# Roots written as transposes, alternating row groups and a reordered start of a hybrid encoder layer

## The chip, the cores and the metric

The kernel runs on one core of a Trainium2 chip. A core has five engines that run side by side, each with its own instruction queue: TensorE (PE, matrix products into the accumulation memory PSUM), VectorE (DVE), ScalarE (ACT), GpSimd (POOL) and SyncE (SP), which here issues all the transfers between the large memory and the on-chip memory. The metric is the device time of one execution in microseconds; the time before is the median of three runs.

## The reference

One inference step of one encoder layer, for a prompt of 2048 new tokens and for a sample of 32 next tokens that sees 2048 cached keys and values. All data are 32-bit floats.

```python
m, k, v, h_fin, ssm_conv_new = mixer(rmsnorm(x, p['g_mix_pre']), k_past, v_past, ssm_h0, ssm_conv_prev, p)
x = x + rmsnorm(m, p['g_mix_post'])
f, ffn_conv_new = conv_ffn(rmsnorm(x, p['g_ffn_pre']), ffn_conv_prev, p)
x = x + rmsnorm(f, p['g_ffn_post'])
```

The mixer projects the normalised tokens (1024 wide) once, to q, k, v, a gate z, the state-space inputs x, B, C and a step size dt. Group A is attention with stick-breaking weights, 8 heads of 64:

```python
log_keep = jnp.where(causal, jax.nn.log_sigmoid(-z), 0.0)
log_after = lax.cumsum(log_keep, axis=3, reverse=True) - log_keep
w = jnp.where(causal, jnp.exp(jax.nn.log_sigmoid(z) + log_after), 0.0)
```

Group B is a state-space scan, 8 heads of 64 in 2 groups, after a causal convolution of width 4 and a SiLU (y times sigmoid of y) on x, B and C. Both outputs are normalised, concatenated and sent through one output projection. The feed-forward part has a hidden width of 2816, a causal convolution of width 3 on the gate branch and a GeLU gate. An RMS norm divides by the root of a token's mean square. Keys, values and states are outputs too.

## The kernel before, in words

Tokens lie along the free dimension and features on the 128 partitions. The 2080 tokens are cut into four chunks (512, 512, 512 and 544, the last with the 32 of the sample behind the prompt's). Every dense product is computed as three products of a high and a low part (`dense`, line 180): high by high, high weight by low input, low weight by high input. A weight comes in raw (`raw`), is cast to its high part on ACT (line 160), has its low part subtracted on POOL (line 161), and is stored to a scratch area (line 164) from which later chunks recall it (line 152).

The first stage, `phase_in`, takes the four chunks s = 0 to 3 in turn. For each chunk:

- The six groups of 128 state-space inputs are projected, copied out of PSUM on ACT (line 412), convolved on DVE (lines 421 and 425) and sent through SiLU (`silu`, lines 397 and 398: a sigmoid on ACT and a product on DVE). The SiLU of a group is owed: it is issued behind the copy of the next group, and the last one behind the first copies of v.
- v and dt are projected in blocks of 128 tokens (line 452, two halves of 260 columns), copied out on ACT (line 459 in the first chunk, 461 in the others), split into high and low parts on POOL (lines 473 and 474, one buffer), and sent out by two kinds of transfer (`o_v`, line 468, and `vS`, line 476). In the first chunk v's weights are loaded before this by `load_wv` in four pieces through one raw buffer (lines 301 to 303: load, cast on ACT, subtraction on DVE). In the later chunks, ahead of the blocks b = 0, 1 and 2, one weight of the output projection each is loaded, split and stored for later use, eight in all.
- The state-space scan runs over blocks of 128 tokens. Line 540 multiplies C and B, line 542 the incoming state by C, each for the two groups g, whose operands lie on partitions 0 to 63 and 64 to 127; the two groups write different banks of the tile `cy`. A 32-bit product that isn't marked for the fast format makes two passes on PE, which the trace shows as two records.
- The next chunk's tokens are loaded (line 318; for chunk 1 the loads are put behind the last raw weight load so far, `kn.load`), normalised, and k and q are projected. In this stage three buffers hold split weights and two hold raw ones.

Then follow the four attention stages, `heads(s)`. A stage walks over slots (head, key chunk, block of 128 queries): scores into PSUM (lines 910 to 914), two sigmoids on ACT (758, 759), a product scan on DVE (761), a product (766), transposes on PE (929), a split on ACT and DVE (933, 934) and the product with v (951). The work of a slot's second half comes two slots behind its scores. Between slots a filler hands out steps of other dense work, at a steady rate that is counted in `debt`. In stage 0 the filler is the last chunk's gate z and its norm, and a generator `sample` is advanced every third slot: it takes the sample's 2048 cached keys in chunks kc = 3 to 0 (and the 32 new ones, kc = 4), loads values (`sv`) and keys (`sk`), makes the scores of two pairs of heads g (line 809), and adds to the sum (line 825). In the stages 1 to 3 the filler is `Tail.stream` of the chunk before: output projection, residual, feed-forward part and final norm; the last chunk's follows alone.

The root of a norm is made in `rstd_steps`: the squares are summed over partitions per token into a column (line 222), the column gets its power of -1/2 on POOL (line 245), and one product per block of 128 tokens (line 257) turns it into rows that are the same on all partitions. The column, repeated over 128 columns, is one operand, the identity matrix the other.

Within each engine's queue the order is set by a planner that takes the program's order as priority and its own estimate of times; `kn.behind(a, b)` and `kn.pin` add edges that keep an instruction behind another.

Of the kernel before, what the change touches and what calls it, by code (L numbers as in the profile page):

```python
# [8 lines left out]
F32 = mybir.dt.float32  # L9
# [8 lines left out]
LOOK = 2  # L18
# [14 lines left out]
P = 128  # L33
D = 1024
KC = D // P
# [4 lines left out]
DH = 64  # L40
# [30 lines left out]
class Kernel:  # L71
# [139 lines left out]
    def rstd_steps(self, pool, psp, pt, sq, n, width, tag="rstd", out=None, rcol=None, of=None, stay=False, pin=False):  # L211
# [3 lines left out]
        nc = self.nc  # L215
# [32 lines left out]
        v = w  # L248
# [3 lines left out]
        for b in range(nb):  # L252
            q = min(P, n - b * P)
            if b == 4:
                nc.scalar.copy(r[:, :512], ps[:])
            c0 = b % 4 * P
            mm = nc.tensor.matmul(
                ps[:, c0 : c0 + q], v[:, b : b + 1].to_broadcast([P, P]), self.ident[:, :q], start=True, stop=True
            )
            if pin and b == 0:  # L260
                self.pin(mm)
        if pin:
# [9 lines left out]
def phase_in(kn, ctx):  # L272
# [8 lines left out]
    wp = kn.wp  # L281
# [16 lines left out]
    def load_wv():  # L298
        for k in range(0, KC, 2):
            raw = ep.tile([P, 2, 520], F32, name="wvraw")  # L300
            nc.sync.dma_start(raw[:], a["wv"][:, k : k + 2, :])
            nc.scalar.copy(wv[0][:, k : k + 2, :], raw[:])
            nc.vector.tensor_tensor(
                wv[1][:, k : k + 2, :], raw[:], wv[0][:, k : k + 2, :].bitcast(F32), op=ALU.subtract
            )
# [70 lines left out]
    for s, (t0, nt) in enumerate(SBS):  # L376
# [12 lines left out]
        if last:  # L389
            nc.vector.tensor_copy(  # L390
                raw[:, :, 515:518], kn.cv[:, C_SST : C_SST + 18].rearrange("p (c t) -> p c t", t=3)
            )
        owed = None

        def silu(y, copy):
            t = tmp.tile([P, 550], F32, name="t")
# [5 lines left out]
        for c, then in zip(order, (*order[1:], None)):  # L402
            if w is None:
                w = kn.weight(wp, a["wbx"][c], key=("bx", c))
            ahead = None
            if s == 0 and then is not None:
                ahead = kn.weight(wp, a["wbx"][then], key=("bx", then))
            for c0, c1 in tiles_of(nt):
                ps = psd.tile([P, 512], F32, name="o")
                kn.dense(ps, w, xs, c0, c1)  # L410
                e = min(c1, 512)
                copy = nc.scalar.copy(raw[:, c, 3 + c0 : 3 + e], ps[:, : e - c0])
                if ahead is not None:
                    kn.behind(copy, kn.cast)
                if c1 > 512:
                    copy = nc.scalar.copy(raw[:, c, 518:550], ps[:, e - c0 : c1 - c0])
            if s == 0:
                nc.vector.tensor_tensor(raw[:, c, 3 : 3 + nt], raw[:, c, 3 : 3 + nt], r0[:, :nt], op=ALU.mult)
            y = xc[:, c, :W] if c < 4 else bc[:, c - 4, :W]
            wc = C_SW + c * 4  # L420
            nc.vector.tensor_scalar(
                y, raw[:, c, 0:W], kn.col(wc), kn.col(C_SB + c), op0=ALU.mult, op1=ALU.add
            )
            for i in range(1, 4):
                nc.vector.scalar_tensor_tensor(  # L425
                    y, raw[:, c, i : i + W], kn.col(wc + i), y, op0=ALU.mult, op1=ALU.add
                )
            if owed is not None:
                silu(owed, copy)
            owed = y  # L430
            w = ahead
        if last:
            nc.sync.dma_start(o["sconv"][0], raw[:, :, 512:515])
# [9 lines left out]
            nc.vector.memset(u[:, 32:40], 0.0)  # L443
        for b in range(nb):
            q = min(P, nt - b * P)
            if 0 < s and b < 3 and 3 * s - 3 + b < KC:
                kn.weight(wp, a["wout"][3 * s - 3 + b], key=("outw", 3 * s - 3 + b))
            vp = [psd.tile([P, 512], F32, name="o") for _ in range(2)]
            for h in range(2):
                for k in range(KC):  # L450
# [9 lines left out]
                else:  # L460
                    copy = nc.scalar.copy(dst, src)
            if b == 0:
                silu(owed, copy)
            nc.vector.tensor_tensor(
                u[:q, b * 8 : b * 8 + 8], v[:q, 512:520], kn.cv[:q, C_DTB : C_DTB + 8], op=ALU.add
            )
# [48 lines left out]
        for b in range(nb):  # L515
# [19 lines left out]
            nc.scalar.activation(eA[:, :, :q], eA[:, :, :q], AF.Exp)  # L535
            h_in = hS if b == 4 else hT[state["h"]]
            cy = psy.tile([P, 2, 512], F32, name="y")
            for g in range(2):
                rows = slice(g * 64, g * 64 + 64)
                nc.tensor.matmul(cy[:q, g, :q], bc[rows, 0, sl], bc[rows, 1, sl], start=True, stop=True)  # L540
                for i in range(2):
                    nc.tensor.matmul(
                        cy[:, g, P + i * q : P + i * q + q],
                        h_in[rows, 2 * i : 2 * i + 2, :].rearrange("p h d -> p (h d)"), bc[rows, 1, sl],
                        start=True, stop=True,
                    )
# [161 lines left out]
class Attention:  # L708
# [60 lines left out]
    def sample(self, ctx, pu):  # L769
# [22 lines left out]
        for kc in (4, 3, 2, 1, 0):  # L792
            n = DEC if kc == 4 else 512
            nsub = 1 if kc == 4 else 4
            v = [kp.tile([P, 512], F32, name="sv", bufs=4) for _ in range(nsub)]
            for i in range(nsub):
                if kc == 4:
                    nc.sync.dma_start(v[i][:DEC, :], kn.vF[:])
# [1 line left out]
                    nc.sync.dma_start(v[i][:], a["cvv"][:, 4 * kc + i, :])  # L800
            for g in range(2):
                z = self.pz.tile([P, 512], F32, name="z")
                for i in range(2):
                    c = 2 * g + i
                    k = kp.tile([P, 512], F32, name="sk", bufs=2)
                    nc.sync.dma_start(
                        k[:, :n], kn.kF[:, c, :] if kc == 4 else a["ck"][c][:, 512 * kc : 512 * kc + 512]
                    )
                    nc.tensor.matmul(
                        z[DH * i : DH * i + DH, :n], qp[:, c, :], k[:, :n], start=True, stop=kc < 4  # L810
                    )
                if kc == 4:
                    nc.tensor.matmul(z[:, :n], kn.identb[:], mk[:], start=False, stop=True)
                w, end = self.weights_of(z[:, :n], n, prev[g], own[g])
# [66 lines left out]
    def heads(self, s, steps, every=None):  # L881
# [3 lines left out]
        slots = [(h, kc, b) for h in range(NH) for kc in range(s, -1, -1) for b in range(4)]  # L885
        att, live, late = [], {}, []
        sq = None
        debt, rate = 0.0, steps / (len(slots) + LOOK)
        cur = {}

        def scores(i):
# [778 lines left out]
```

## Time and profile before

| | |
|---|---|
| median of 3 runs | 2902.88 us (2899.2 to 2905.06) |
| the profiled execution | 2897.34 us |
| its span, first to last instruction | 2895.5 us |
| mean granted TensorE clock | 0.985 |
| busy: PE, DVE, ACT, POOL | 97%, 57%, 42%, 39% of the span |
| moved by transfers | 642.04 MB, mean 222 GB/s |

In the lines of the profile an instruction is named by its line in the kernel, its engine, its operation and its tiles (out<-in). A group's row has the count (x), the busy time and the mean length of one. A row of a list of one line has the shortest, middle and longest length in ns, then the first and last start. A row of a timeline has the start and the length in us, and in brackets how long the engine was idle before it and what ended that. Matmuls are pipelined: the length of one record is longer than the distance to the next. `o`, `u`, `z`, `pt`, `pa`, `st` and `y` are PSUM tiles, `w<-wraw` is a weight's split, `w<-wS_...` a recalled weight.

### The profile page before, as it was taken

How to read it: one execution, taken by the hardware profiler on the slowest of the kernel's cores; microseconds unless marked ns; L12 is line 12 of the kernel's file. 1: busy time of each engine (PE TensorE's matmuls, PEld its weight loads, DVE VectorE, ACT ScalarE, POOL GpSimd, SP SyncE). 2: the span in 40 equal slices, each digit the busy share in tenths (PEclk: the TensorE clock that was granted, in tenths of full speed). 3: DMA queues.
4: the chain of work that ended last, by engine and by line, in shares of the span. 5: the costliest groups of instructions: out<-in, count | busy, mean ns of one | idle time of the engine just before them, and what ended most of it. 6: DMA issues, size and time to landing. Idle time of an engine off the chain costs nothing.

```text
span 2895.5 us, 46167 instructions
## 1 busy us (share of the span) xinstructions
PE 2798.5 (97%) x16771; PEld 2416.4 (83%) x16771; DVE 1651.0 (57%) x2628; ACT 1217.8 (42%) x2568; POOL 1134.5 (39%) x1065
## 2 busy tenths in 40 slices
PE   7999999988999999999999999989999999999998
PEld 6878789976978888887888888978888889999997
DVE  7594747367564554557555555785666653623333
ACT  4343434246555454455433334654444443321111
POOL 3534242224566666556322223453223323511113
PEclk9999999999999999999999999999999999999999
DMA  8889695878767787875755556666555555755566
GB/s 291 269 303 304 240 305 206 244 227 263 233 232 265 273 273 253 274 257 192 227 169 182 183 179 227 207 202 196 172 168 171 167 176 184 249 178 178 170 177 204
DMA packets 348644, 642.04 MB, mean 222 GB/s; under 512 B 73498, under 2 KB 192930, under 8 KB 338690
## 3 DMA queue, kind: packets, MB, share of 16 engines
q1 hardware_dynamic: 348418, 639.09, 67.9%
q8 instruction: 134, 2.20, 0.3%
q14 instruction: 92, 0.75, 0.1%
HBM read 482.40 MB, written 156.57 MB: 221 GB/s over the span
## 4 chain that ended last, share of the span: by engine, by line
PE 77%; DVE 11%; DMA 6%; issue 3%; ACT 2%; POOL 1%; SPq 1%; DVEq 0%; ACTq 0%; POOLq 0%
PE o L180 39%; PE u L180 12%; PE t L180 11%; PE z L910 4%; PE pa L951 4%; PE pt L929 4%; DVE xc L425 2%; PE o L452 1%; DMA acB<-acD 1%; DVE prow L761 1%; DVE xlo L1099 1%; DVE f L1427 1%; DMA vS<-vs 1%; DMA o_kT<-kf 1%; PE u L222 1%
## 5 line engine op out<-in xcount | busy, mean ns | idle before, releaser
L180 PE MATMUL o<-xhi,w 128*128 128x512 f32 (+2 forms) x3968 | 1041.2, 344 | 17.9 <-ACT xhi L355 7.7
L180 PEld LDWEIGHTS o<-xhi,w 128*128 128x128 f32 x3968 | 694.4, 191 | 111.1 <-ACT xhi L355 7.7
L180 PE MATMUL o<-xlo,w 128*128 128x512 f32 (+2 forms) x1984 | 679.7, 343 | 1.5 <-DVE xlo L356 1.1
L766 POOL TENSOR_TENSOR beta<-beta,prow 128x512 f32<-128x512 f32 (+3 forms) x256 | 255.9, 1000 | 511.1 <-DVE prow L761 427.9
L180 PEld LDWEIGHTS o<-xlo,w 128*128 128x128 f32 x1984 | 377.6, 190 | 44.4 <-DVE xlo L356 1.6
L180 PE MATMUL u<-xhi,w 128*128 128x512 f32 x1056 | 351.3, 398 | 0.0
L180 PE MATMUL o<-ah,w 128*128 128x512 f32 x992 | 342.7, 402 | 3.4 <-DVE f L1395 3.3
L161 POOL TENSOR_TENSOR w<-wraw,w 128x512 fp32r<-128x512 f32 (+3 forms) x178 | 243.1, 1368 | 155.2 <-ACT w L160 127.8
L1347 POOL TENSOR_TENSOR y<-y,gb 128x512 f32<-128x512 f32 (+1 forms) x88 | 116.0, 1318 | 457.7 <-ACT gb L1346 457.4
L934 DVE TENSOR_TENSOR wt<-pt,wt 128x512 fp32r<-128x512 f32 (+2 forms) x320 | 191.6, 601 | 155.0 <-ACT wt L933 153.0
L761 DVE TENSOR_TENSOR_SCAN prow<-gam,prow,z 128x513 f32<-128x513 f32 x192 | 245.0, 1277 | 58.4 <-ACT beta L759 58.1
L933 ACT CAST wt<-pt 128x512 fp32r<-128x512 f32 (+2 forms) x320 | 167.3, 525 | 237.8 <-PE pt L929 235.9
L180 PEld LDWEIGHTS u<-xhi,w 128*128 128x128 f32 x1056 | 198.6, 188 | 46.2
L180 PEld LDWEIGHTS o<-ah,w 128*128 128x128 f32 x992 | 187.1, 189 | 45.8 <-DVE f L1395 4.4
L180 PE MATMUL u<-xlo,w 128*128 128x512 f32 x528 | 209.1, 396 | 0.0
L758 ACT ACTIVATE gam<-z 128x512 f32<-128x512 f32 (+2 forms) x320 | 173.0, 541 | 66.0 <-PE z L910 40.0
L180 PE MATMUL o<-al,w 128*128 128x512 f32 x496 | 196.7, 396 | 0.0
L180 PE MATMUL t<-xhi,w 128*128 128x272 f32 x960 | 189.4, 293 | 3.3 <-DMA w<-wS_outw 2.1
L929 PE MATMUL pt<-ident,beta 128*128 128x128 f32 x1088 | 182.8, 277 | 4.7 <-DVE wt L934 4.6
L1339 DVE SCALAR_TENSOR_TENSOR y<-gb,cv,y 128x512 f32<-128x512 f32 (+1 forms) x176 | 143.2, 813 | 69.1 <-ACT y L1337 66.0
L951 PE MATMUL pa<-wt,v 128*64 128x256 f32 (+3 forms) x1152 | 173.2, 281 | 7.7 <-DVE wt L934 5.5
L160 ACT CAST w<-wraw 128x512 fp32r<-128x512 f32 (+3 forms) x178 | 113.0, 635 | 158.5 <-PE o L180 93.1
(288 smaller groups left out, 4907.6 us busy)
## 6 DMA issues: line engine op xcount, KB each, us to landing
w<-wS_up SPq DMA_DIRECT2D x264, 512.0 KB, 3.5
w<-wS_dn SPq DMA_DIRECT2D x144, 384.0 KB, 3.5
w<-wS_outw SPq DMA_DIRECT2D x94, 512.0 KB, 6.2
wS_up<-w SPq DMA_DIRECT2D x88, 512.0 KB, 3.6
wraw<-wup SPq DMA_DIRECT2D x88, 256.0 KB, 4.2
k<-kS SPq DMA_DIRECT2D x80, 256.0 KB, 3.8
v<-vS SPq DMA_DIRECT2D x80, 256.0 KB, 3.7
w<-wS_bx SPq DMA_DIRECT2D x18, 1024.0 KB, 5.3
```

Of the source, the lines that this page charges most:

```text
L161: nc.gpsimd.tensor_tensor(lo, raw[:, :m, :], hi.bitcast(F32), op=ALU.subtract)
L180: mm = nc.tensor.matmul(ps[:, : c1 - c0], l, r, start=first and i == 0 and k == 0, stop=last and i == 2 and k == len(w) - 1, **({"skip_gro ...
L758: nc.scalar.activation(g[:, c0:512], z, AF.Sigmoid, scale=-0.125)
L761: nc.vector.tensor_tensor_scan(back(pr), back(g), z[:, 0:1].to_broadcast([P, n + 1]), self.kn.ones[:, 0:1] if prev is None else prev, op0= ...
L766: eng.tensor_tensor(b[:, :n], b[:, :n], pr[:, c0 + 1 : 513], op=ALU.mult)
L910: mm = nc.tensor.matmul(z[:, :n], q[:, P * b : P * b + P], k[:, :n], start=e == 0, stop=e == 1 and kc < s)
L929: mm = nc.tensor.transpose(t[:, P * j : P * j + P], w[:, P * j : P * j + P], kn.ident[:])
L933: nc.scalar.copy(hi, t)
L934: kn.exit = nc.vector.tensor_tensor(lo, t, hi.bitcast(F32), op=ALU.subtract)
L951: nc.tensor.matmul(av[:m, 2 * P * p + c0 : 2 * P * p + 2 * P], v[:, j, :m], wt[:, rest, j, c0:], start=kc == s and p + j + rest == 0, stop ...
L1339: nc.vector.scalar_tensor_tensor(y[:, :W], gb[:, i : i + W], kn.col(wc + i), y[:, :W], op0=ALU.mult, op1=ALU.add)
L1347: nc.gpsimd.tensor_tensor(y[:, :W], y[:, :W], t, op=ALU.mult)
```

## The change

There are seven edits. In `rstd_steps` the product with the identity becomes a transpose of the repeated column. In `phase_in`, `load_wv` notes its loads in `kn.load`, so that the loads of chunk 1's tokens stand behind the last of v's weights; two SiLUs are owed and not one, and the two that remain come behind v's first copies; the output weights come one block later (ahead of the blocks 1, 2 and 3), with their cast on ACT behind the copies of v before it; and the products of the two row groups alternate. In `sample` one transfer brings the keys of both halves of a pair, the scores are made in pieces of 256 columns that alternate between the halves, and `sv` has eight tiles and not four. In `heads(0)` the filler starts with four steps of credit.

```diff
-            mm = nc.tensor.matmul(
-                ps[:, c0 : c0 + q], v[:, b : b + 1].to_broadcast([P, P]), self.ident[:, :q], start=True, stop=True
-            )
+            mm = nc.tensor.transpose(ps[:, c0 : c0 + q], v[:q, b : b + 1].to_broadcast([q, P]), self.ident[:q, :q])
...
-            nc.sync.dma_start(raw[:], a["wv"][:, k : k + 2, :])
+            kn.load = nc.sync.dma_start(raw[:], a["wv"][:, k : k + 2, :])
...
-        owed = None
+        owed = []
...
-            if owed is not None:
-                silu(owed, copy)
-            owed = y
+            if len(owed) == 2:
+                silu(owed.pop(0), copy)
+            owed.append(y)
...
-            if 0 < s and b < 3 and 3 * s - 3 + b < KC:
-                kn.weight(wp, a["wout"][3 * s - 3 + b], key=("outw", 3 * s - 3 + b))
+            if 0 < s and 0 < b < 4 and 3 * s + b < KC + 4:
+                kn.weight(wp, a["wout"][3 * s - 4 + b], key=("outw", 3 * s - 4 + b))
+                kn.behind(kn.cast, copy)
...
             if b == 0:
-                silu(owed, copy)
+                for y in owed:
+                    silu(y, copy)
...
-            for g in range(2):
-                rows = slice(g * 64, g * 64 + 64)
+            half = [slice(g * 64, g * 64 + 64) for g in range(2)]
+            for g, rows in enumerate(half):
                 nc.tensor.matmul(cy[:q, g, :q], bc[rows, 0, sl], bc[rows, 1, sl], start=True, stop=True)
-                for i in range(2):
+            for i in range(2):
+                for g, rows in enumerate(half):
                     nc.tensor.matmul(
...
-            v = [kp.tile([P, 512], F32, name="sv", bufs=4) for _ in range(nsub)]
+            v = [kp.tile([P, 512], F32, name="sv", bufs=8) for _ in range(nsub)]
...
-                for i in range(2):
-                    c = 2 * g + i
-                    k = kp.tile([P, 512], F32, name="sk", bufs=2)
-                    nc.sync.dma_start(
-                        k[:, :n], kn.kF[:, c, :] if kc == 4 else a["ck"][c][:, 512 * kc : 512 * kc + 512]
-                    )
-                    nc.tensor.matmul(
-                        z[DH * i : DH * i + DH, :n], qp[:, c, :], k[:, :n], start=True, stop=kc < 4
-                    )
+                k = kp.tile([P, 2, 512], F32, name="sk", bufs=2)
+                src = kn.kF[:, 2 * g : 2 * g + 2, :]
+                if kc < 4:
+                    src = a["ck"][2 * g : 2 * g + 2, :, 512 * kc : 512 * kc + 512].rearrange("c p n -> p c n")
+                nc.sync.dma_start(k[:, :, :n], src)
+                for c0 in range(0, n, 256):
+                    c1 = min(n, c0 + 256)
+                    for i in range(2):
+                        nc.tensor.matmul(
+                            z[DH * i : DH * i + DH, c0:c1], qp[:, 2 * g + i, :], k[:, i, c0:c1],
+                            start=True, stop=kc < 4,
+                        )
...
-        debt, rate = 0.0, steps / (len(slots) + LOOK)
+        debt, rate = 4.0 * (s == 0), steps / (len(slots) + LOOK)
```

## The prediction

> **What bounds the kernel now.** I read the page first, then busy time by stretch, then the timelines of TensorE (PE), ScalarE (ACT), VectorE (DVE) and GpSimd (POOL) around every pause of PE.
>
> ```profile
> span 2895.5 us, 46167 instructions
> PE 2798.5 (97%) x16771; PEld 2416.4 (83%) x16771; DVE 1651.0 (57%) x2628; ACT 1217.8 (42%) x2568; POOL 1134.5 (39%) x1065
> PE 77%; DVE 11%; DMA 6%; issue 3%; ACT 2%; POOL 1%; SPq 1%; DVEq 0%; ACTq 0%; POOLq 0%
> 0.00:600.00 600.00, 569.86 (x3489) 483.14 (x3489) 382.72 (x708) 236.51 (x397) 223.63 (x165) 0.99 0.80 266
> 600.00:745.00 145.00, 127.93 (x898) 102.63 (x895) 99.29 (x166) 87.07 (x220) 61.97 (x80) 0.91 0.76 241
> ```
>
> The last two rows are stretches: start and end, length, busy time of PE, weight loads, DVE, ACT and POOL with counts, granted clock, DMA share, GB/s. PE is busy 97% of the span and is 77% of the chain of waits, so a TensorE pass that disappears is worth about its own start-to-start time, and a pause of PE about its length. The pauses are early: 30 us in the first 600 us (input projections and state space), 17 us in the 145 us after it (first attention stage and the sample), there with a granted clock of 0.91. All edits but the first lie in those stretches.
>
> **Roots by transposes.** Each root is a column turned into a row by one product per 128 tokens.
>
> ```profile
> L257 PE MATMUL u<-ident,rn_v x108: 182/275/486, 732.1 to 2886.2; 128*128 128x128 f32 x96, 128*128 128x16 f32 x12
> L257 PE MATMUL u<-ident,rn_w x36: 182/275/275, 790.8 to 2486.8; 128*128 128x128 f32 x32, 128*128 128x16 f32 x4
> L257 PE MATMUL st<-ident,rn_v x34: 192/275/376, 30.9 to 450.7; 128*128 128x128 f32 x32, 128*128 128x32 f32 x2
> L257 PE MATMUL o<-ident,rn_v x10: 241/275/276, 690.8 to 693.3; 128*128 128x128 f32 x8, 128*128 128x32 f32 x2
> 690.76 1.06 PE L257 MATMUL o<-ident,rn_v 128*128 128x128 f32 x8
> 691.65 0.49 PE L929 MATMUL pt<-ident,beta 128*128 128x128 f32 x3
> 734.60 0.60 PE L929 MATMUL pt<-ident,beta 128*128 128x128 f32 x4
> 735.04 0.58 PE L222 MATMUL u<-ones,sq 128*128 128x1 f32 x4
> ```
>
> The four 128-token blocks of one root made eight records (690.76), two passes a block, 0.89 us until the next line: 0.111 us a pass. A transpose of the attention (line 929) is one record, and four of them take 0.44 us (734.60 to 735.04): 0.11 us each. There are 108+36+34+10 = 188 records, so 94 passes go: at most 10.4 us. The narrow blocks save less and some roots end where PE waits anyway; I take 8.5, with 0 and 10.4 as bounds.
>
> The Trainium skill speaks against this edit: "TensorE: Matmul & The Clock Gate", section "Part 4: PE-mode transpose", gives about 275 ns for a transpose inside a kernel and says that transposes do not count as activity for the clock. By its figure 94 transposes would be an estimated 26 us. The trace has that duration for a single record (275 ns in the middle at line 257, 0.60 us for four transposes at 734.60), but the spacing is 0.11 us.
>
> **State-space rows alternate.** The twelve passes of a block on two halves of the rows get a new order.
>
> ```profile
> 142.63 1.09 PE L580 MATMUL y<-acB,xdt 128*64 128x128 f32 x16
> 143.65 0.48 PE L540 MATMUL y<-bc 64*128 64x128 f32 x2
> 143.98 0.27 PE L542 MATMUL y<-bc,hT 64*128 64x128 f32 x1
> 143.98 0.37 PE L540 MATMUL y<-bc 64*128 64x128 f32 x1
> ...
> 144.84 0.74 PE L180 MATMUL o<-xhi,w 128*128 128x512 f32 x2
> ```
>
> The block takes 1.19 us (143.65 to 144.84), 0.099 us a pass. Line 580, which already alternates halves of the columns, takes 1.02 us for sixteen, 0.064 us a pass. At that rate twelve passes save 0.42 us; four chunks have four blocks each: 6.7 us. But the halves overlap partly today (two passes both begin at 143.98), so I take 5, bounds 0 and 6.7. The two halves write different banks of the tile, so no new wait arises.
>
> **v's weights ahead of the next tokens, and two activations owed.** The first block of v stops PE twice:
>
> ```profile
> 58.62 0.39 PE L452 MATMUL o<-wvhi,xhi 128*128 128x260 f32 x1 [3.90 <-ACT wvhi L302]
> 63.77 0.59 PE L452 MATMUL o<-wvlo,xhi 128*128 128x260 f32 x1 [4.26 <-DVE wvlo L303]
> 57.51 1.05 ACT L302 CAST wvhi<-wvraw 128x1040 fp32r<-128x1040 f32 x1
> 62.48 1.24 DVE L303 TENSOR_TENSOR wvlo<-wvraw,wvhi 128x1040 fp32r<-128x1040 f32 x1
> 60.00:64.00 4.00, 0.23 (x1) 0.23 (x2) 3.96 (x5) 0.63 (x1) 0.57 (x1) 0.50 0.77 261
> 64.00:70.00 6.00, 6.00 (x31) 6.00 (x32) 2.02 (x5) 3.46 (x6) 3.11 (x4) 0.56 0.66 191
> 76.00:82.00 6.00, 6.00 (x52) 6.00 (x52) 0.17 (x1) 2.09 (x5) 3.55 (x3) 1.00 1.03 306
> ```
>
> The idle times are 3.90 and 4.26 us, and the clock is at 0.50 to 0.56 until 70: 31 passes in six us where 52 run later, 21 x 6/52 = 2.4 us more. All of it is 10.6 us. Moving the next tokens' four loads behind the fourth load of v's weights clears the DMA engines for it, but the cast at 57.51 and the subtraction at 62.48 stand in queues whose other work stays, with one buffer between loads. Owing two activations takes one wait out of ACT's queue. I take 5; bounds 0 and 10.6. The moved loads land before the squares that use them, which ACT does after v's first copies; without that slack they would cost a landing.
>
> Later chunks:
>
> ```profile
> 358.57 0.63 ACT L397 ACTIVATE t<-xc 128x512 f32<-128x512 f32 x1 [4.68 <-DVE xc L425]
> 359.52 0.39 PE L452 MATMUL o<-wvhi,xhi 128*128 128x260 f32 x1 [1.86 <-ACT v L461]
> 213.65 0.39 PE L452 MATMUL o<-wvhi,xhi 128*128 128x260 f32 x1 [1.80 <-ACT v L461]
> ```
>
> In chunks 2 and 3 a sigmoid waits 4.68 us for DVE with v's first copies queued behind it, and PE waits 1.86 and 1.80 us for those copies. With two owed, this sigmoid stands behind the copies: 3.5 us, bounds 0 and 3.7. Chunk 4's stop stays: there the copy waits for an output transfer and not for the sigmoid.
>
> **Output weights behind v's copies.** Eight weights, each cast on ACT, subtracted on POOL and stored, move into the stretch of v's blocks.
>
> ```profile
> 205.74 5.53 POOL L161 TENSOR_TENSOR w<-wraw,w 128x1024 fp32r<-128x1024 f32 x2 [4.04 <-ACT w L160]
> 230.42 0.61 POOL L473 CAST vs<-v 128x512 fp32r<-128x512 f32 x1 [1.78 <-DMA vS<-vs]
> 232.41 0.65 ACT L461 COPY v<-o 128x260 f32<-128x260 f32 x2 [5.59 <-POOL vs L474]
> w<-wS_wk SPq DMA_DIRECT2D x12, 1024.0 KB, 8.6
> wS_outw<-w SPq DMA_DIRECT2D x8, 1024.0 KB, 4.9
> 1010.40 5.60 PE o L180 x24
> ```
>
> POOL needs 2.77 us for one. Today two end before v's first split; afterwards they stand between the splits, on which the copy at 232.41 waits 5.59 us. The bounds are a gain of 1.78 us a chunk (5.3), if the transfer waited for at 230.42 no longer shares the queue with a weight's store, and a loss of 8 x 2.77 = 22 us, if every subtraction holds up a copy. Nearest is the row at 230.42, where the split waits for a transfer and not for POOL, so most is hidden: a loss of 1.5.
>
> **The sample and the head start.**
>
> ```profile
> 634.65 1.07 PE L809 MATMUL z<-sk,qp 128*64 128x512 f32 x2 [0.71 <-DMA sk<-ck]
> 688.60 1.08 PE L809 MATMUL z<-sk,qp 128*64 128x512 f32 x4
> 698.36 1.04 PE L809 MATMUL z<-sk,qp 128*64 128x512 f32 x2 [2.34 <-DMA sk<-ck]
> 605.46 0.69 PE L910 MATMUL z<-k,qa 128*128 128x384 f32 x1 [2.15 <-DVE prow L761]
> 606.00:612.00 6.00, 6.00 (x25) 4.93 (x24) 3.37 (x5) 2.58 (x7) 3.61 (x7) 0.50 0.81 226
> ```
>
> Where both halves of a pair are there, four passes take 1.08 us (688.60); one half alone takes 1.07. Five of the eight full pairs ran apart, first at 634.65, last at 698.36: about 1.0 us each, 5.0; the two waits for the transfer add 3.05. One load per pair and twice the tiles for its values remove both; splitting into 256 columns keeps the work. This stretch also waits for DVE scans, which stay, so of 8 I take 5; bounds 0 and 8.
>
> Four filler steps (24 matmuls) in front can cover the 2.15 us at 605.46 and spare the half clock, at which 25 matmuls took six us and not three: up to 5.1. The same 24 are then missing later, 3 us. I take 1.5, bounds -3 and 5.1.
>
> **Sum.** 8.5 + 5 + 5 + 3.5 - 1.5 + 5 + 1.5 = 27 us. The profiled execution took 2897.3 us (the span and 1.8 around it), so 2870; it lay 5.5 us under the median of 2902.9, so the median becomes 2876. All upper ends together, 50 us, give 2853.
>
> **Rivals.**
> - Only removed passes count (roots and rows, 13.5 us). The pauses move: v's copies to the splits (5.59 us at 232.41), the sample to the scans. That gives 2889. For it: DVE is busy 99 of 145 us there; against: PE itself names the waits.
> - The three weight buffers decide, the slower side. An output weight cast late holds a buffer for cast, subtraction and store, about 1 + 2.8 + 4.9 = 8.7 us, while k and q need a new weight every 5.60 us that takes 8.6 us to land. With one buffer short, PE waits 3.1 us for the buffer and 3.0 for the landing: 6 x 8 = 48 us, so 2903 - 28.5 + 48 = 2923. It outweighs the gains from 3.6 us a weight. Against: no wait of PE for these loads is among the long ones now.
> - Transposes of a broadcast column don't overlap, each taking the 275 ns that a record of line 257 lasts: 26 us where the passes took 20.9, so 5 lost and not 8.5 won: 2889. Against: 0.11 us spacing at 734.60. This is the skill's rule of above.
> - The change doesn't do what it says: a planner sets the order, and ordering edits that shift its times may return elsewhere what they save: 2903, within 0.2%.
>
> **How the numbers follow.** Forecast 0.58, only passes 0.22, buffers 0.08, slow transposes 0.04, planner 0.08. A measurement of this kernel can tell about 0.2% (5.8 us) from no change. Faster: 0.58 + 0.22 + 0.04 = 0.84; same 0.08; slower 0.08. The range 2854 to 2900 takes in the upper ends, the second and fourth case, and part of the last.
>
> **What would show it.** Line 257: half as many records, spaced 0.11 us. Lines 540 and 542: a block of twelve under 0.9 us. No idle of 3.90 and 4.26 us at line 452, full clock by 64 us. No wait of about 1.8 us for v's copies in chunks 2 and 3. Line 809: eight passes of 256 columns together, no wait for sk. No pause at the third score, and a clock above 0.91 in that stretch. I am wrong if PE waits for recalled k or q weights, if v's copies wait longer for POOL, or if new pauses of like length stand where the old ones went.

## The result and the profile after

The changed kernel takes 2888.57 us (median of 5 runs, 2885.98 to 2891.35), the kernel before in the same comparison 2899.2 us: a ratio of 0.9961, interval 0.9948 to 0.9974. That is 11 us or 0.4% faster. The direction was forecast, the size was not: 27 us were expected. Below, a ratio is turned into microseconds with 2898 us, about the median of the kernel before in every comparison; a ratio's interval is about 0.0012 or 3.5 us to each side.

The page of the changed kernel:

```profile
span 2885.6 us, 46011 instructions
PE 2780.3 (96%) x16709; PEld 2401.0 (83%) x16709; DVE 1643.5 (57%) x2628; ACT 1217.0 (42%) x2568; POOL 1134.0 (39%) x1065
PE 79%; DMA 8%; DVE 7%; issue 2%; SPq 2%; POOL 1%; ACT 1%; DVEq 0%; ACTq 0%; POOLq 0%
```

PE's busy time fell by 18.2 us (2798.5 to 2780.3), the span by 9.9. Nearly half of the work that went has come back as time in which PE waits, and DMA rose from 6% to 8% of the chain of waits. Busy time by stretch, after (columns as in the prediction):

```profile
0.00:600.00 600.00, 565.98 (x3476) 476.61 (x3476) 379.76 (x698) 237.76 (x400) 223.78 (x166) 0.99 0.80 268
600.00:745.00 145.00, 130.89 (x1014) 112.77 (x1015) 99.31 (x178) 89.69 (x228) 66.89 (x87) 0.91 0.82 263
60.00:64.00 4.00, 3.91 (x30) 3.70 (x31) 4.00 (x7) 1.58 (x3) 2.15 (x2) 1.00 1.02 425
...
600.00:606.00 6.00, 4.43 (x31) 4.33 (x32) 3.92 (x16) 1.19 (x3) 1.99 (x8) 0.53 0.79 200
```

The clock is full at 60 us, as hoped, but the first 600 us still hold 34 us without PE (30 before). The first score starts at 602.6 us, where it started at 602.5 before, with the same products in front of it but for the 17 root passes that went: what the first stage won is gone by then. One execution tells this start only to some 3 us: in the five kernels that have the first stage of the kernel before (it, and the kernels below that change nothing ahead of the first score) it lies between 598.4 and 603.6. PE's timeline, after:

```profile
53.12 0.49 PE L540 MATMUL y<-bc 64*128 64x128 f32 x4 [2.78 <-DVE bc L396]
...
59.98 0.39 PE L451 MATMUL o<-wvlo,xhi 128*128 128x260 f32 x1 [1.56 <-DVE wvlo L301]
...
139.58 0.49 PE L540 MATMUL y<-bc 64*128 64x128 f32 x4
139.91 0.61 PE L543 MATMUL y<-bc,hT 64*128 64x128 f32 x8
140.45 0.38 PE L222 MATMUL st<-ones,sq 128*128 128x1 f32 x2
...
228.50 0.77 PE L180 MATMUL o<-xhi,w 128*128 128x512 f32 x1 [3.92 <-DMA w<-wS_wk]
...
378.24 0.53 PE L180 MATMUL o<-xhi,w 128*128 128x512 f32 x1 [3.42 <-DMA w<-wS_wk]
...
634.20 1.08 PE L812 MATMUL z<-sk,qp 128*64 128x256 f32 x8
635.21 0.33 PE L933 MATMUL pt<-ident,beta 128*128 128x128 f32 x1
```

The stops of 3.90 and 4.26 us for v's weights at the first v block are gone; 2.78 and 1.56 us stand there now, the first of them for the SiLU of `bc` (line 396), which is owed longer than before. A state-space block takes 0.87 us (139.58 to 140.45) and not 1.19. Eight pieces of a pair of sample scores run in 1.01 us. The 1.80 and 1.86 us for v's copies are gone, but 3.92 and 3.42 us for a recalled k weight stand 15 to 19 us behind. In the list of PE's waits, after, those for k and q weights are new, and two have grown: `f` (3.3 us before) and the up weight in `t` (1.2 before):

```profile
PE o L180 <- DMA w<-wS_wk: 7.3, 2, 3.9
PE o L180 <- DVE f L1399: 6.3, 5, 2.8
...
PE t L180 <- DMA w<-wS_up: 4.6, 1, 4.6
...
PE o L180 <- DMA w<-wS_wq: 3.0, 2, 2.1
```

Columns: total, times, longest. PE waits 10.3 us for recalled k and q weights. The groups of instructions of line 257 and of the sample's scores (line 809 before, 812 after), first the kernel before, then the changed one:

```profile
L809 PE MATMUL z<-sk,qp 128*64 128x512 f32 x32 | 13.9, 616 | 4.5 <-DMA sk<-ck 3.0 <-DMA k<-kS 1.3
```

```profile
L257 PE MATMUL u<-ident,rn_v 128*128 128x128 f32 x48 | 9.8, 288 | 3.7 <-POOL rn_v L245 3.7
...
L812 PE MATMUL z<-sk,qp 128*64 128x256 f32 x64 | 8.9, 398 | 0.0
```

The roots have half their records (48 here for 96). The sample's scores take 8.9 us for 13.9, and 4.5 us of waits in front of them are gone.

### The profile page after: what moved, and what is told of

Same layout as the page of the kernel before. It is cut to its first block, busy times and chain, and to the rows that moved or that the text cites. A ratio compares the mean times of both kernels' runs of the same rounds, so it can differ in the third digit from the quotient of the medians.

```text
span 2885.6 us, 46011 instructions
## 1 busy us (share of the span) xinstructions
PE 2780.3 (96%) x16709; PEld 2401.0 (83%) x16709; DVE 1643.5 (57%) x2628; ACT 1217.0 (42%) x2568; POOL 1134.0 (39%) x1065
## 4 chain that ended last, share of the span: by engine, by line
PE 79%; DMA 8%; DVE 7%; issue 2%; SPq 2%; POOL 1%; ACT 1%; DVEq 0%; ACTq 0%; POOLq 0%
PE o L180 41%; PE u L180 12%; PE t L180 10%; PE z L914 4%; PE pa L955 4%; PE pt L933 4%; PE o L451 2%; DMA acB<-acD 1%; DMA w<-wS_outw 1%; DVE prow L762 1%; DMA w<-wS_wk 1%; DMA w<-wS_up 1%; DVE f L1431 1%; DVE xlo L1103 1%; DMA k<-kS 1%
```

## The experiments

After the result there were two theories. The first: the late output weights took back what the first stage won, and everything else counts. The second: what one part wins comes back through the order that the planner writes or through the next wait. Each kernel here is the kernel before plus some parts, or the changed kernel less some; one has a fourth buffer.

| kernel | ratio to before | interval | us |
|---|---|---|---|
| changed kernel | 0.9961 | 0.9948 to 0.9974 | -11.3 |
| roots alone | 1.0009 | 0.9996 to 1.0021 | +2.6 |
| roots outside the first stage alone | 1.0000 | 0.9990 to 1.0011 | 0 |
| v's weights noted, two owed, alone ("start") | 1.0009 | 0.9997 to 1.0021 | +2.6 |
| rows alternate alone | 0.9996 | 0.9985 to 1.0008 | -1.2 |
| late output weights alone | 1.0051 | 1.0037 to 1.0066 | +14.8 |
| head start alone | 1.0042 | 1.0028 to 1.0057 | +12.2 |
| sample alone | 0.9969 | 0.9957 to 0.9980 | -9.0 |
| of it, pairs alone | 0.9969 | 0.9957 to 0.9981 | -9.0 |
| of it, eight value tiles alone | 1.0000 | 0.9990 to 1.0010 | 0 |
| roots and sample | 0.9985 | 0.9973 to 0.9997 | -4.3 |
| rows and sample | 0.9971 | 0.9961 to 0.9981 | -8.4 |
| start, rows and sample | 0.9960 | 0.9948 to 0.9973 | -11.6 |
| changed, without the sample part | 1.0012 | 1.0001 to 1.0023 | +3.5 |
| changed, without the roots | 0.9989 | 0.9979 to 0.9999 | -3.2 |
| changed, output weights early | 0.9956 | 0.9944 to 0.9968 | -12.8 |
| changed, without the head start | 0.9961 | 0.9948 to 0.9975 | -11.3 |
| changed, without both of these | 0.9963 | 0.9950 to 0.9977 | -10.7 |
| changed, four split-weight buffers | 0.9981 | 0.9971 to 0.9991 | -5.5 |

### The output weights

The part undone, and the part alone:

```diff
-            if 0 < s and 0 < b < 4 and 3 * s + b < KC + 4:
-                kn.weight(wp, a["wout"][3 * s - 4 + b], key=("outw", 3 * s - 4 + b))
-                kn.behind(kn.cast, copy)
+            if 0 < s and b < 3 and 3 * s - 3 + b < KC:
+                kn.weight(wp, a["wout"][3 * s - 3 + b], key=("outw", 3 * s - 3 + b))
```

> The changed kernel with one part undone: the output weights are issued and cast before the products of each chunk again, as before. Theory 1 (the late output weights hold split-weight buffers and POOL, so that the recalled k and q weights come late and take back the 6 us that the first stage won and the 2 to 8 us of each later chunk): about 2877 us, 10 to 12 us under the changed kernel's 2888.6; no wait of 3 to 4 us for a k weight at the head of a chunk (228.50 and 378.24 now), and the first score starts 6 us or more before that of the kernel before (602.54). Theory 2 (no single part is at fault: the gains come back through the order that the planner finds): within 5 us of 2888.6, and the first score within 3 us of 602.5.

> The kernel before with one part of the change alone: the output weights issued at later blocks and cast behind the copies of v. Theory 1: 8 to 13 us slower than the kernel before (2907 to 2912), with waits for recalled k weights of 3 to 4 us. Theory 2: within 3 us of it (2896 to 2902).

Alone, the part costs 14.8 us, somewhat over the 8 to 13 of the first theory. Undone in the changed kernel, it gives back 1.5 us, which can't be told from nothing, where 10 to 12 were expected. The waits for k weights do go: PE's waits between 195 and 615 us, in the kernel with the part alone, and in the changed kernel with the part undone:

```profile
PE y L581 <- DVE acB L553: 6.3, 4, 2.5
...
PE o L180 <- DMA w<-wS_wk: 3.4, 2, 2.2
```

```profile
PE o L450 <- ACT v L459: 7.1, 3, 2.9
```

With the part undone the first score starts 6.0 us sooner (596.7), and no k weight is waited for; the waits for v's copies stand in their place (7.1 us). Of the 6 us the profiled execution keeps 3.5 at its end (a span of 2882.1 us) and the median 1.5. So the wait of the first theory is there, and its price in the whole is wrong. In the kernel with the part alone it is not even the larger share: the first score starts 13.6 us later than before (616.1), and k weights are 3.4 us of PE's waits there, DVE's `acB` 6.3.

What holds the k weight was tried with a fourth buffer:

```diff
-            kn.wp, kn.unit, kn.wbufs, kn.rbufs = c2.enter_context(tc.tile_pool(name="weights_in", bufs=1)), KC, 3, 2
+            kn.wp, kn.unit, kn.wbufs, kn.rbufs = c2.enter_context(tc.tile_pool(name="weights_in", bufs=1)), KC, 4, 2
```

> The changed kernel with four split-weight buffers in place of three up to the first score. Theory 1 (the cast that stands behind v's copy holds a buffer, and the recalled k weight waits for it): the waits of 3.9 and 3.4 us for the k weight at the head of chunks 1 and 2 are gone, the first score starts 5 to 8 us sooner, and 2 to 8 us of it are left at the end. Theory 2 (the k weight is late because SP or POOL is, not the buffer): the waits stay within 1 us of what they are, and the time within 3 us of the changed kernel's.

It is 5.8 us slower than the changed kernel (with some 5 us to each side), its first score starts no sooner (604.0), and two waits for a k weight stay, 5.9 us together. SP's timeline, in the kernel before, in the changed kernel and with four buffers, and PE's wait there:

```profile
209.39 0.85 SPq L152 DMA_DIRECT2D w<-wS_wk  x1
...
214.38 0.52 SPq L468 DMA_DIRECT2D o_v<-v  x1
```

```profile
218.87 0.34 SPq L468 DMA_DIRECT2D o_v<-v  x1
219.31 1.22 SPq L152 DMA_DIRECT2D w<-wS_wk  x1
```

```profile
217.07 0.34 SPq L468 DMA_DIRECT2D o_v<-v  x1
217.50 2.28 SPq L152 DMA_DIRECT2D w<-wS_wk  x2
...
225.34 0.47 PE L180 MATMUL o<-xhi,w 128*128 128x512 f32 x1 [2.57 <-DMA w<-wS_wk]
```

Before, the recall of the first k weight is issued at 209.39, ahead of an output transfer of v. In the changed kernel it stands behind one in SP's queue, with three buffers and with four: at 219.31, and at 217.50 with the fourth, each 0.4 us behind `o_v`. What SP's queue waited for between 205 and 232 us, in the changed kernel:

```profile
SPq L468 <- ACT v L460: 16.4, 3, 11.0
...
SPq L152 <- DMA wS_outw<-w: 2.1, 1, 2.1
```

Line 468 is `o_v`, which waits for copies of v, and the recall (line 152) stands behind it; the recall's own wait, for the store of an output weight, is 2.1 us, the buffer's part. With the fourth buffer PE waits 1.35 us less at this place. So, as these timelines read, the order of SP's queue sets the time of this load, and the buffer a smaller part; no kernel with the recall put ahead of `o_v` and nothing else changed was run.

### The roots

```diff
-            mm = nc.tensor.matmul(
-                ps[:, c0 : c0 + q], v[:, b : b + 1].to_broadcast([P, P]), self.ident[:, :q], start=True, stop=True
-            )
+            mm = nc.tensor.transpose(ps[:, c0 : c0 + q], v[:q, b : b + 1].to_broadcast([q, P]), self.ident[:q, :q])
```

> The kernel before with the roots by transposes alone (94 fewer fp32 passes). If every pass that goes counts (94 at 0.11 us, or 90 us per thousand less): 8.5 to 10 us faster. If the passes lie in stretches where PE then waits for the same work, or if the planner's order gives it back: 3 us faster or less.

Page and list of PE's waits with the roots alone, and lines of the list of the kernel before:

```profile
PE 2788.2 (96%) x16677; PEld 2403.3 (83%) x16677; DVE 1657.3 (57%) x2628; ACT 1217.3 (42%) x2568; POOL 1133.5 (39%) x1065
```

```profile
PE z L908 <- DVE prow L759: 14.3, 18, 2.6
...
PE o L180 <- DVE f L1393: 6.3, 5, 2.8
PE o L450 <- ACT wvhi L300: 5.4, 1, 5.4
PE o L450 <- DVE wvlo L301: 5.3, 1, 5.3
...
PE t L180 <- DMA w<-wS_up: 4.1, 2, 3.4
```

```profile
PE z L910 <- DVE prow L761: 9.6, 12, 2.2
...
PE o L452 <- DVE wvlo L303: 4.3, 1, 4.3
PE o L452 <- ACT wvhi L302: 3.9, 1, 3.9
PE o L180 <- DVE f L1395: 3.3, 4, 1.4
...
PE t L180 <- DMA w<-wS_up: 1.2, 1, 1.2
```

94 records went (16771 to 16677) and 10.3 us of PE's busy time, 0.11 us a pass, just as worked out. The time did not move. PE's idle time rose by 13.4 us (97.0 to 110.4, the span less PE's busy time). Five waits grew by 13.1 us together: 4.7 for the scans, 3.0 for `f`, 1.5 and 1.0 for v's weights, 2.9 for a recalled up weight in `t` (one for the up weight in `o` fell, from 2.6 to 1.0; others moved both ways). The wait for `f` is no accident of one execution: it is 6.3 us in each of the nine kernels here that have all or most of the transposes, and 2.3 to 3.4 in the other eleven. The edit touches one instruction of PE, but the planner then wrote the queues anew. Compared row by row, the built program with the roots alone has hundreds of rows of PE's queue, and tens to hundreds on every other engine, elsewhere than the kernel before; the head start does the same, and the late output weights and the start come near it on PE. The pairs of the sample move tens of rows on PE, and the row groups move rows of PE alone: there the other four queues are the same.

> The kernel before with the roots by transposes outside the first stage alone (77 of the 94 passes, 8.5 us at 0.11 us), so that the instructions of the first stage keep the order that they had. If it was the new order of the first stage that took the gain (v's weights 2.7 us later, the sample's first scores 2 to 5 us later): 5 to 8.5 us faster than the kernel before. If the late roots' time comes back as pauses where PE then waits for vector work or weights: within 3 us.

With `if pt == "st"` the products stay in the first stage and 77 passes go elsewhere. The time is that of the kernel before, and the wait for the up weight is longer still. PE's timeline there:

```profile
2514.33 0.56 PE L180 MATMUL t<-xhi,w 128*128 128x272 f32 x1 [5.27 <-DMA w<-wS_up]
```

So the first stage's new order is not the cause, or not the only one: near the end PE comes sooner to a weight that does not come sooner (the product starts at 2514.33 us after 5.27 idle, before at 2515.76 after 1.20).

> The changed kernel with the roots by products again (94 passes more, 10 us of PE's busy time). If the roots' passes count there: 5 to 10 us slower than the changed kernel (0.998 to 0.9995 of the kernel before). If their time comes back as pauses there too: within 3 us of it (0.995 to 0.997).

In the changed kernel, though, the roots are worth 8 us (0.9989 without, 0.9961 with; both intervals together leave about 5 us to each side). On top of the sample part alone they are worth nothing, less than either theory allowed:

> The kernel before with two parts: the roots by transposes and the sample part. The sample part alone gave 0.997 and the roots alone 1.001, with 10 us less of PE's busy time that came back as waits. If the roots' passes can count once the sample stretch is shorter: 0.993 to 0.994. If their time always comes back: 0.997.

That pair comes out 4.6 us slower than the sample part alone (with some 5 us to each side). And start, rows and sample together (0.9960, below) differ by the roots alone from the changed kernel without the late output weights and the head start (0.9963): there they are worth nothing either. One edit, four surroundings, between 8 us won and 5 us lost.

One more thing bears on this term, which the prediction named and gave no price: the granted clock. In each of the five comparisons that differ by the roots alone, its mean over the executions is lower with the transposes:

| | without | with |
|---|---|---|
| kernel before | 0.9848 | 0.9827 |
| the same, roots outside the first stage | 0.9846 | 0.9834 |
| sample part | 0.9862 | 0.9818 |
| start, rows and sample | 0.9862 | 0.9838 |
| changed kernel | 0.9848 | 0.9834 |

The last is at the edge of the noise. Taken as shares of 2898 us the differences are an estimated 4 to 13 us, of the size of what the passes save. Whether the transposes themselves or PE's longer pauses lower the clock, no run separates; the late output weights alone lower it too (0.9830), with no transpose added.

### Rows

```diff
+            half = [slice(g * 64, g * 64 + 64) for g in range(2)]
-            for g in range(2):
-                rows = slice(g * 64, g * 64 + 64)
+            for g, rows in enumerate(half):
                 nc.tensor.matmul(cy[...
-                for i in range(2):
+            for i in range(2):
+                for g, rows in enumerate(half):
```

> The kernel before with the state-space rows alternating alone. If each pair that now starts together counts: about 5 us faster than the kernel before. If the passes of the two halves mostly overlapped already, or PE then waits for the work that it came to sooner: within 2 us.

This is the cleanest case, since the queues of the four other engines are the same row by row. Most blocks take 0.87 us in place of 1.19, and the work of a later block, at 587.2 us before, begins at 583.0. By 600 us some 4.5 us are won (by the spread of the first score, 3 us to each side). PE's waits between 590 and 720 us, before and with rows alone:

```profile
PE z L809 <- DMA sk<-ck: 3.0, 2, 2.3
...
PE z L809 <- DMA sk<-kF: 2.3, 1, 2.3
PE z L809 <- DMA k<-kS: 1.3, 1, 1.3
```

```profile
PE z L810 <- DMA sk<-kF: 3.5, 1, 3.5
PE z L810 <- DMA sk<-ck: 3.5, 3, 2.5
PE z L810 <- DVE xc L698: 3.2, 1, 3.2
```

Before the sample's scores PE now waits 10.2 us where it waited 6.6. That is 3.6 of the 4.5 us. PE comes sooner to products whose keys and vector work come no sooner: the first score starts 5.2 us sooner (597.3), the last product with the sample's keys 0.6 (708.1 and 708.7).

### Start

> The kernel before with two parts alone: v's weights noted ahead of the next tokens, and two owed sigmoids in place of one. Theory 1 (the stops for v's weights and v's copies were on the path, and only the late output weights take their place): about 9 us faster (6 in the first stage, 3 at the later chunks). Theory 2 (the first stage's gain is lost later whatever the output weights do): within 3 us of the kernel before.

```diff
-            nc.sync.dma_start(raw[:], a["wv"][:, k : k + 2, :])
+            kn.load = nc.sync.dma_start(raw[:], a["wv"][:, k : k + 2, :])
-            if owed is not None:
-                silu(owed, copy)
-            owed = y
+            if len(owed) == 2:
+                silu(owed.pop(0), copy)
+            owed.append(y)
```

5 us are won at 101 us in its trace, 2.4 of them are left at the sample's first full chunk of keys, 0.4 at its last and none at 770 us. The end is no sooner. The waits for v's copies, which the second owed SiLU was to take away, stay in this kernel: 2.69 and 2.16 us (at 213.72 and 360.65) where 1.80 and 1.86 stood before. They are gone only where the output weights come late.

### The sample and the head start

> The kernel before with the sample part alone: eight value tiles, two loads of the sample's keys in one, 256-column scores. Theory 1 (nearly all of the 11 us comes from the sample's stretch, 602 to 716 us, which the changed kernel runs 12 us faster from the same first score, 602.6): 8 to 12 us faster than the kernel before. Theory 2 (the stretch is shorter because the planner starts the ordinary units sooner, with the head start; the sample part alone gives back what it wins): within 3 us of the kernel before.

> The changed kernel with the sample part undone. Theory 1: 8 to 12 us slower than the changed kernel, so within 3 us of the kernel before. Theory 2: within 3 us of the changed kernel, 8 to 11 us faster than the kernel before.

Alone the sample part gives 9.0 us, 80% of the whole result. Without it the changed kernel is no faster than the kernel before. It was then cut in two:

```diff
-                for i in range(2):
-                    k = kp.tile([P, 512], F32, name="sk", bufs=2)
...
+                k = kp.tile([P, 2, 512], F32, name="sk", bufs=2)
+                nc.sync.dma_start(k[:, :, :n], src)
+                for c0 in range(0, n, 256):
+                    c1 = min(n, c0 + 256)
+                    for i in range(2):
```

> The kernel before with the sample's keys in one load per pair and the scores in alternating 256-column pieces, its value tiles still four. If the passes carry the part: 6 to 9 us faster than the kernel before. If the loads do: within 3 us.

```diff
-            v = [kp.tile([P, 512], F32, name="sv", bufs=4) for _ in range(nsub)]
+            v = [kp.tile([P, 512], F32, name="sv", bufs=8) for _ in range(nsub)]
```

> The kernel before with eight value tiles for the sample and nothing else. If the earlier loads carry the part: 5 to 9 us faster. If the passes do: within 3 us.

The pairs are all of it; the eight value tiles do nothing. Groups and page with the pairs alone:

```profile
L811 PE MATMUL z<-sk,qp 128*64 128x256 f32 x64 | 8.9, 393 | 0.3 <-DVE prow L761 0.3
L811 PE MATMUL z<-sk,qp 128*64 128x32 f32 x8 | 0.7, 265 | 5.4 <-DMA sk<-kF 5.4
```

```profile
PE 2788.2 (97%) x16803; PEld 2414.5 (84%) x16803; DVE 1652.0 (57%) x2628; ACT 1219.1 (42%) x2568; POOL 1138.0 (39%) x1065
```

The scores take 5.0 us less. This edit holds both the one load and the narrower pieces, so the runs don't separate them, but the trace of the kernel before does: there three pairs had both halves ready together, with 512 columns a product.

```profile
688.60 1.08 PE L809 MATMUL z<-sk,qp 128*64 128x512 f32 x4
689.48 1.07 PE L825 MATMUL u<-sv,swt 128*64 128x128 f32 x16
```

Such a pair took 0.88 us, and with the pairs alone eight pieces take 0.92 (647.12 to 648.04). So it is the one load, which lets every pair run together, and not the pieces of 256 columns.

Of the waits at the scores 4.2 us are gone (4.5 to 0.3), but the one wait for the new keys grew by 3.1; PE's idle time as a whole is 98.8 us, 1.8 more than before, where the roots alone raised it by 13.4. PE's busy time is 10.3 us lower, as with the roots alone, and here the span of the profiled execution falls by 8.5. Two things in that execution are not the scores: its first score starts 3.5 us sooner (599.1), with nothing changed ahead of it, and its clock between 600 and 745 us is 0.96, not 0.91, about 7 us of that stretch. Over all executions the mean clock is 0.9857, and 0.9846 before, a difference within the noise. The 9.0 us of the medians don't rest on that one execution; how they divide between the passes, the waits and the clock stays open.

> The kernel before with the planner's head start alone (four steps owed at the first score). Theory 1: within 3 us of the kernel before (the pause at the third score, 1 to 2 us, is all it can win). Theory 2: 5 to 11 us faster.

```diff
-        debt, rate = 0.0, steps / (len(slots) + LOOK)
+        debt, rate = 4.0 * (s == 0), steps / (len(slots) + LOOK)
```

The head start alone moves the same work in another order and costs 12.2 us. In its profiled execution (7.0 us above the one before; it lay 5.6 under its own median) the stretch from 770 to 1330 us holds most of that loss; busy times there, before and with the head start:

```profile
770.00:1330.00 560.00, 545.23 (x2908) 455.51 (x2906) 313.70 (x434) 302.29 (x671) 348.78 (x330) 0.98 0.78 262
```

```profile
770.00:1330.00 560.00, 540.79 (x2892) 454.67 (x2892) 309.70 (x426) 297.88 (x661) 343.60 (x326) 0.98 0.78 259
```

PE is busy 4.4 us less in 560, hundreds of us behind the four steps that were moved. Nor do the steps cover the pause that they were meant for: with the head start alone the third score (601.30 us) still waits 2.15 us for DVE's scan, as before. In the changed kernel the pause is gone, but it is gone without the head start too (the score at 607.13 us there starts with no wait).

> The changed kernel with the planner's head start undone. Theory A (each part carries its own price wherever it stands; the head start alone made the kernel before 12 us slower): 8 to 12 us faster than the changed kernel, 0.992 of the kernel before or less. Theory B (what a part costs depends on the order that the planner then writes, and the sample's shorter stretch is where the head start's work goes): within 4 us of the changed kernel's 0.996.

> The changed kernel with both parts undone that alone made the kernel before slower: the output weights early as before, no head start. Theory A: 20 us or more under the kernel before, 0.993 or less. Theory B: 8 to 15 us under it, near 0.996.

In the changed kernel the same edit costs nothing, and undoing both costly parts brings nothing either. So theory B holds for these two parts: what they cost belongs to the order in which they stand.

### Combinations

> The kernel before with two parts: alternating rows and the sample part. If the first stage's gain was lost only in the pauses in front of the sample's scores (613, 632 and 698 us, 3.8 us longer with rows alone): it counts now, 0.9969 less 4 us, so 0.9955 or less. If any sooner start of the sample is lost in that stretch, whoever ends it: 0.997 as with the sample part alone.

> The kernel before with the start (v's weights noted, two owed sigmoids), rows and sample: the changed kernel without the roots, the late output weights and the head start. If the first stage's gains count once the sample part is there: 9 + 4.5 + 3 us, so 2881 us, 0.994. If they are lost: 0.996 to 0.997.

Rows add nothing to the sample part. Start, rows and sample together reach 0.9960, the case in which the first stage's gains are lost, and the same as the changed kernel with all of its parts. No kernel here is measurably faster than the changed one: the five at 0.9956 to 0.9963 can't be told apart.

## Why the prediction was right or wrong

The time lay inside the range and on the side that was forecast. What failed is the first rule of the sum, that "a TensorE pass that disappears is worth about its own start-to-start time, and a pause of PE about its length". The terms for passes were sized well as work (10.3 us of PE's busy time for the roots, 5 for the rows), but that work was not time: alone these parts gave no gain. PE's next waits grew by about as much (13.4 us of idle time with the roots, 3.6 in front of the sample with the rows). That the time still fell inside the range, near its slow end, owes nothing to the sum, it is luck: one part, the sample, gives nearly all of it alone.

- **Roots, 8.5.** 94 records fewer and 0.11 us each, as worked out; 10.3 us of busy time. Worth nothing alone (2.6 us slower, within the noise), 8 us won inside the whole. The clock, which the term put at nothing, is lower with the transposes in all five comparisons. The rival of slow transposes is out: busy time falls by 0.11 us a pass, and the Trainium skill's 275 ns ("TensorE: Matmul & The Clock Gate", "Part 4: PE-mode transpose") shows here as the length of a record, not as its cost in the stream.
- **Rows, 5.** 16 blocks at 0.32 us less are 5.1 us. Alone 1.2 us, which can't be told from nothing; 3.6 us came back in front of the sample's scores.
- **First block of v and later chunks, 5 and 3.5.** The stops shrank: 3.90 and 4.26 to 2.78 (for a later SiLU) and 1.56 us, and the clock was full at 60 us. The first stage was 5 us ahead at 101 us, and that comes to nothing at the end. For the later chunks the mechanism itself was wrong: two owed SiLUs alone leave the waits for v's copies (2.69 and 2.16 us); it is the late output weights that take them away.
- **Output weights, -1.5.** 14.8 us lost alone, inside the bound of 22 but ten times the value taken. The row chosen (the split that waits for a transfer) spoke of POOL. The waits that came in the changed kernel are for k and q weights, by its timeline through SP: v's output transfer stands ahead of the k weight's recall in one queue. With the part alone that is 3.4 us, and most of the loss is not traced. The text named the sign, "I am wrong if PE waits for recalled k or q weights", and PE does, 10.3 us. In the whole it costs about 1.5 us, in the order that it finds there.
- **Sample, 5.** Undersized: 9.0. Of its parts the 5.0 for passes is what was measured. Of the 3.05 for the transfer the waits at the full chunks went (4.2 us), but 3.1 came back at the new keys. The value tiles, which it counted with the load, do nothing.
- **Head start, 1.5.** It does not cover the pause at the third score: alone the 2.15 us stay, and in the changed kernel the pause is gone with it or without it. The clock between 600 and 606 us was still 0.53. Alone 12.2 us lost, outside the bound of -3, which priced only the missing cover and not a new order.
- **The rivals.** The number, 2889, is that of "only removed passes count", but its mechanism is wrong: roots and rows alone are worth nothing. The slow transposes gave 2889 too; that the time is theirs shows nothing. "The three weight buffers" had the right wait, at 10 us and not 48, and the wrong holder. "The change doesn't do what it says" had the mechanism: ordering edits return elsewhere what they save. It was given 0.08, and without the sample part it would have come true (1.0012).

Added up, the six parts alone make 22 us slower (2.6 + 2.6 - 1.2 + 14.8 - 9.0 + 12.2). Together they are 11 us faster. No sum over parts could have been right, with true prices either.

What stays open: which rows of the new order make 12 us of the head start, what most of the late output weights' loss is, why the roots count inside the whole, and how much of any of this is the clock. The order of one kernel could not be given to another, so order and content of a part were not separated except for the rows.

## What to carry to other kernels

On an engine that is 97% busy, a pass saved is worth time only if what it runs into next comes sooner too: look for the next wait behind the place. The one edit that paid alone, the paired load, cut passes without adding to PE's waits on balance. Where a planner writes the queues, compare the queues before the times: the parts here that move hundreds of rows missed their price by 11 to 14 us, and even the rows, which leave the other engines' queues alone, gave 1 us of 5. Compare the mean granted clock of all executions too, and not of the profiled one alone. Time every part alone and by undoing it in the whole: here the two differ by up to 13 us.

## What was not expected of the hardware

Two products on opposite halves of the rows start 6 to 7 ns apart when they stand next to each other (the block at 139.58 us), so that twelve passes take 0.87 us. The same holds for the halves of the columns, and the width of the pieces doesn't matter there: four passes of 512 columns take 0.88 us and eight of 256 columns 0.92, while a half that stood alone took about 1.0 us for itself, so that the sample's scores fell from 13.9 to 8.9 us for the same number of columns. And the mean granted clock was lower by 0.0012 to 0.0044 in each of the five pairs of kernels above that differ only in whether the roots are transposes; why, no run shows.
